# A two-layer hybrid transformer on one Trainium2 core: the delta rule's first doubling, the order of short TensorE products, and the convolution tiles

## The chip, the core and the metric

The kernel runs on one core of a Trainium2 chip. The metric is the device time of one execution in microseconds (us), as the median of several runs.

## The reference

Two layers, each made of a half-weighted SwiGLU, a mixer and a second half-weighted SwiGLU, with a layer norm after each. Layer 0 has the hybrid mixer (a gated delta rule beside a state-space scan), layer 1 the NSA mixer (compressed, selected and windowed attention). 256 tokens, width 1024, all in float32.

```python
def reference(...):
    h = x
    for layer in range(DEPTH):                       # DEPTH = 2
        h = layer_norm(ALPHA * h + 0.5 * swiglu(h, ffn_w_in[layer, 0], ffn_w_out[layer, 0]), ...)
        mix = hybrid_mixer(h, ...) if layer % 2 == 0 else nsa_mixer(h, positions, ...)
        h = layer_norm(ALPHA * h + mix, ...)
        h = layer_norm(ALPHA * h + 0.5 * swiglu(h, ffn_w_in[layer, 1], ffn_w_out[layer, 1]), ...)
    return h

def hybrid_mixer(x, w_in, ...):
    proj = x @ w_in                                  # split: gdn q,k,v | gdn z | b | a | ssd z | ssd x,B,C | dt
    o_a = gdn_branch(...)                            # silu(causal_conv(q,k,v)), then the gated delta rule
    o_b = ssd_branch(...)                            # silu(causal_conv(x,B,C)), then the scan
    return jnp.concatenate([o_a, o_b], axis=-1) @ w_out

# in gated_delta_rule, per head and chunk of tokens:
    a_low = where(strict lower triangle, (k * beta) @ k.T * decay, 0)
    sol = triangular_solve(a_low, rhs, lower=True, unit_diagonal=True)     # inverse of I + a_low
```

The causal convolution has four taps: each channel's output is a weighted sum of its projection at the token and the three before.

## The kernel before

Every weight is split into two fp32r parts, `whi` (rounded) and `wlo` (the rest), and so is the activation `x`. A float32 product is then three products on TensorE: high by high, high by low, low by high. The split is a ScalarE copy (or VectorE, as the planner decides) and a VectorE subtraction for each 128x1024 tile of weights.

**The planner.** No instruction is issued where it is written. A call like `nc.tensor.matmul` only records an operation (`Plan.add`). `Plan.order` then simulates all engines and picks, again and again, the operation that can start first, and among those of one engine that could start at once the one with the lowest priority number (its place in the recording). `price` is its cost table, `TURN` what it charges when TensorE goes from full to partial products (weights of 64 or fewer rows or columns). `Plan.emit` issues them in that order, which is why every row of the profile has one line, the line in `emit`. So a change of a price moves instructions and computes nothing else.

**The recording order** of a mixer comes from `weave`: it takes generators and always advances the one whose recorded TensorE cost divided by its weight is smallest. `W_HYB` are the weights for the hybrid's five: `delta` (delta rule), `space` (convolutions of v and of the state space), `gate` (the state space's z), `space2` (its scan), `out_a` (the first half of the output projection); `A_HYB` are head starts. `W_NSA` and `A_NSA` are those of the NSA mixer. `ORDER` adds random numbers to the priorities of a stage, here stage 4, the NSA mixer.

**Convolution tiles.** The hybrid has 28: 8 for q and k (`gdn_conv`, not woven with anything), 8 for v, 12 for the state space (both in `space`). A tile is 128 channels by 256 tokens, held in a PSUM bank, mostly `ps`, of which there are two. `proj_steps` computes it in 8 steps of three products of 256 columns. `conv_tile` then copies the bank to SBUF (`src`, part of a tile `cv`) on ScalarE, scales it by the last tap, adds the other three taps with three VectorE instructions, and applies SiLU on ScalarE.

**The inverse.** `delta` inverts 16 unit lower triangular 128x128 matrices (8 heads, two chunks) by doubling. Forward substitution on VectorE gives the inverses of all 16x16 diagonal blocks, `W`. From it two tiles are built: `Yd` (the inverse blocks) and `Xd` (their transposes), halves of one tile `XY` (`D2` in the code). The first doubling goes from 16x16 to 32x32 blocks with three sets of 64 products of 32x32 weights and 16 columns (four partition groups by 16 matrices): `pT` from the matrix and `Xd`, then `pY` and `pX` from `pT`, which correct `Yd` and `Xd`. In the profile they are `acc<-XY,AT`, `acc<-XY,TT` and `acc<-TT,XY` with 32x16. Each float32 product is two rows of the profile, each with a weight load. The next doublings (32x32 columns, then 64x64) follow in the same way.

**The start.** `spin(4, 4)` issues two products of 512 columns on ones, which nobody reads, while the first transfers are under way.

Of the kernel before, what the change touches and what calls it, by code (L numbers as in the profile page):

```python
# [45 lines left out]
    4: [(59170, 5.0, 1)],  # L46
}

ENDS = 3

# [8 lines left out]
A_HYB, A_NSA = (0.0, 10.0, 0.0, 0.0, 0.0), (0.0, -10.0, 0.0, -10.0)  # L59
W_HYB, W_NSA = (49.0, 114.0, 27.0, 19.0, 14.0), (122.0, 85.0, 81.0, 28.0)  # L60
# [127 lines left out]
class Op:  # L188
    __slots__ = ("eng", "fn", "args", "kw", "idx", "prio", "cost", "table", "deps", "succ", "ndep", "ready", "start",
                 "end", "alloc", "dense", "alts", "tiles", "nbytes", "quad", "port", "banks", "hot")  # L190


class Plan:
# [83 lines left out]
    def price(self, op, eng, fn, args, kw):  # L277
# [3 lines left out]
        if eng == "tensor":  # L281
            out, l, r = args[:3]
            if fn == "transpose":
                return max(l.ids.size * 2, r.ids.size) / 2.4 + 2
            N, M = r.ids.size, l.ids.size
            if l.dtype == F32R:
                return N / 2.4 + (13.5 if M > 32 else 7)
            if M <= 32:
                return N * 0.42 if l.p1 - l.p0 > 32 else max(20.0, N * 1.3)
            if M <= 64:  # L290
                return 58.0 if N <= 64 else max(109.0, N * 0.84)
            return 4 * max(N, M) / 2.4 + 9
# [63 lines left out]
    TURN = 150.0  # L356
# [3 lines left out]
    def order(self, caps):  # L360
        ops = self.ops
        for op in ops:
# [9 lines left out]
            op.banks = [] if op.eng == "tensor" else [t for t in op.tiles if t.space == "PSUM"]  # L372
            op.dense = op.eng == "tensor" and op.args[1].dtype == F32R and op.args[2].ids.size >= 256
# [17 lines left out]
        recent = []  # L391
        order = []
# [63 lines left out]
        while left:  # L456
            best = None
            for e in engs:
# [6 lines left out]
                for op in lst:  # L465
# [8 lines left out]
                    if e == "tensor":  # L474
                        if op.quad != partial:
# [24 lines left out]
            if eng == "tensor":  # L500
                partial = op.quad
                l, r = args[1:3]
# [95 lines left out]
class K:  # L598
# [307 lines left out]

    def proj_steps(self, x, w, ps):
# [328 lines left out]
    def conv_tile(self, ps, cw, off, n, c, bias, dst):  # L1236
# [5 lines left out]
        nc.scalar.activation(src, ps, AF.Copy)  # L1242
        self.plan.ops[-1].prio -= RANK
# [61 lines left out]
    def hybrid(self, x, then):  # L1305
# [75 lines left out]
        def gdn_conv(dests, banks=("ps", "ps")):  # L1381
            for n in range(0, len(dests), 2):
                w = self.col_tiles([w_col[c] for c, _ in dests[n:n + 2]])
                for e in range(2):
                    c, dst = dests[n + e]
                    ps = self.bank(banks[e])[:, :T]
                    yield from self.proj_steps(x, w[e], ps)
# [37 lines left out]
        def delta():  # L1425
# [56 lines left out]
            sw.append(self.m4(1024, "sw2"))  # L1482
            for w, dst, t in ((W, Yd, sw[0]), (W.rearrange("p r c -> p c r"), Xd, sw[2])):
                a, c = t[:, :512], t[:, 512:]
                for e in range(2):
                    V.tensor_scalar(a4(a)[:, :, e, :], w, hm[:, e:e + 1], None, OP.mult)
                V.transpose(c, a)
                self.copy(dst.rearrange("p k (a r) -> p k a r", a=2), c.rearrange("p (r a k) -> p k a r", r=16, a=2))
# [4 lines left out]
            yield  # L1493
            pT = self.bank("acc")
            for b, h, k in heads:
                for q in QS:
                    nc.tensor.matmul(pT[q, k * 16:k * 16 + 16], AT[b][q, h, q], Xd[q, k, :16], start=True, stop=True)
            V.tensor_scalar(Tt[:, :, :16], H3(pT[:, :256], 16), hm[:, 1:2], None, OP.mult)
            yield
            pX, pY = (t[:, :256] for t in (self.bank("acc"), self.bank("acc")))  # L1500
            for b, h, k in heads:
                for q in QS:
                    nc.tensor.matmul(pY[q, k * 16:k * 16 + 16], Tt[q, k, :], Yd[q, k, 16:], start=True, stop=True)
            for b, h, k in heads:
                for q in QS:
                    nc.tensor.matmul(pX[q, k * 16:k * 16 + 16], Yd[q, k, :], Tt[q, k, :16], start=True, stop=True)
            V.tensor_tensor(Yd[:, :, 16:], Yd[:, :, 16:], H3(pY, 16), OP.subtract)
            V.tensor_tensor(Xd[:, :, :16], Xd[:, :, :16], H3(pX, 16), OP.subtract)
# [3 lines left out]
            for b, h, k in heads:  # L1512
# [771 lines left out]
```

## Time and profile before

| what | value |
|---|---|
| median of 3 runs | 1071.63 us (1070.99 to 1073.05) |
| the profiled execution: its own time | 1072.49 us |
| the profiled execution: span in the profile | 1070.8 us |
| TensorE products (PE) busy | 1053.1 us, 98% |
| VectorE (DVE) busy | 1005.8 us, 94% |
| ScalarE (ACT) busy | 728.8 us, 68% |
| mean granted TensorE clock | 0.995 |

PE is TensorE's products, PEld its weight loads (they overlap), DVE is VectorE, ACT ScalarE, POOL GpSimd. Start times are in us from the start of the span. Products are pipelined, so the recorded length of one (283 ns for 256 columns) is longer than the distance to the next; costs below are taken from distances between starts. "<-issue" as the end of an idle time means that the profile shows nothing that was waited for.

### The profile page before, as it was taken

Reading aid. Unit: us, or ns where it says so; the run is one execution under the profiler, and the core shown is the slowest. Engines: PE = TensorE matmul, PEld = TensorE weight load, DVE = VectorE, ACT = ScalarE, POOL = GpSimd, SP = SyncE. Lnnn points to the kernel's source line nnn. Section 1 sums busy time; section 2 is a strip of 40 time slices with the busy share of each in tenths; the row PEclk is TensorE's granted clock in tenths of the full one; section 3 lists DMA queues with packets and bytes.
Section 4 is the critical chain, followed back from the end, with each engine's and each line's share of the span. In section 5 each row is a group of like instructions: output and inputs, shape, how many; then the busy total and the mean of one; then the engine's idle time right before and its main releaser. Section 6 shows DMA issues by size and latency. Waiting matters only on the chain.

```text
span 1070.8 us, 16409 instructions
## 1 busy us (share of the span) xinstructions
PE 1053.1 (98%) x6068; PEld 883.3 (82%) x6068; DVE 1005.8 (94%) x1433; ACT 728.8 (68%) x1162; POOL 70.6 (7%) x115
## 2 busy tenths in 40 slices
PE   9999999999989999999999999999999999999997
PEld 6888887898979888888887888888888778888885
DVE  6999999889979999999998999999988989999996
ACT  6678866389646765568875676678565887666770
POOL 0000000002001310000000000000101000000000
PEclk9999999999989999999999999999999999999999
DMA  9688867535522674378767647778662436477861
GB/s 369 225 274 237 254 220 278 176 115 206 161 99 91 217 254 176 135 252 257 233 221 254 212 142 237 230 240 266 207 222 69 151 112 222 148 228 233 258 194 40
DMA packets 64497, 217.30 MB, mean 203 GB/s; under 512 B 8560, under 2 KB 11296, under 8 KB 64416
## 3 DMA queue, kind: packets, MB, share of 16 engines
q1 hardware_dynamic: 59952, 200.25, 53.6%
q0 software_dynamic: 4320, 15.73, 8.2%
q8 instruction: 48, 0.79, 0.3%
q10 hardware_dynamic: 144, 0.26, 0.1%
q14 instruction: 33, 0.27, 0.1%
HBM read 213.96 MB, written 1.07 MB: 201 GB/s over the span
## 4 chain that ended last, share of the span: by engine, by line
PE 88%; DVE 6%; DMA 2%; ACT 1%; issue 1%; POOL 0%; SPq 0%; DVEq 0%; POOLq 0%; ACTq 0%
PE ps L574 42%; PE acc L574 32%; PE mp L574 14%; DVE wlo L574 1%; DMA raw<-in_hyb_w_tok_dram 1%; DVE arena L574 1%; DVE cv L574 1%; DMA DT<-rows 1%; DVE o L574 1%; DVE qs L574 0%; DMA X<-in_x_cols_dram 0%; ACT whi L574 0%; POOL arena L574 0%; ACT cv L574 0%; SPq L574 0%
## 5 line engine op out<-in xcount | busy, mean ns | idle before, releaser
L574 DVE TENSOR_TENSOR wlo<-raw,whi 128x1024 fp32r<-128x1024 f32 (+3 forms) x417 | 491.1, 1209 | 7.6 <-ACT whi L574 6.8
L574 ACT ACTIVATE whi<-raw 128x1024 fp32r<-128x1024 f32 (+2 forms) x430 | 429.5, 1047 | 89.0 <-DVE raw L574 73.2
L574 PE MATMUL ps<-whi,x 128*128 128x512 f32 (+1 forms) x864 | 233.5, 388 | 0.0
L574 PEld LDWEIGHTS ps<-whi,x 128*128 128x128 f32 x864 | 157.0, 188 | 29.1 <-issue 0.8
L574 DVE TENSOR_TENSOR raw<-raw,raw 128x1024 f32<-128x1024 f32 x128 | 152.6, 1218 | 0.0
L574 PE MATMUL ps<-wlo,x 128*128 128x512 f32 (+1 forms) x432 | 129.6, 387 | 0.0
L574 PE MATMUL ps<-x,whi 128*128 128x256 f32 (+2 forms) x560 | 115.8, 314 | 0.1
L574 PE MATMUL acc<-whi,gh 128*128 128x512 f32 x253 | 98.4, 392 | 0.6 <-ACT gh L574 0.6
L574 PE MATMUL acc<-whi,gl 128*128 128x512 f32 x253 | 98.4, 391 | 0.0
L574 PEld LDWEIGHTS ps<-x,whi 128*128 128x128 f32 (+1 forms) x560 | 91.6, 190 | 7.8 <-ACT cv L574 1.6
L574 PEld LDWEIGHTS ps<-wlo,x 128*128 128x128 f32 x432 | 79.3, 188 | 14.2 <-DVE wlo L574 0.2
L574 PE MATMUL acc<-wlo,gh 128*128 128x512 f32 x253 | 84.9, 391 | 0.0
L574 PE MATMUL ps<-x,wlo 128*128 128x256 f32 (+1 forms) x344 | 79.9, 285 | 0.0
L574 PE MATMUL acc<-whi,x 128*128 128x512 f32 x224 | 74.2, 408 | 1.0 <-ACT whi L574 1.0
L574 POOL DMA_DIRECT2D wlo<-in_ffn_w_out_dram x30 | 26.2, 873 | 555.8 <-ACT wlo L574 272.3
L574 PE MATMUL acc<-whi,g 128*128 128x512 f32 x192 | 61.0, 393 | 0.0
L574 PEld LDWEIGHTS ps<-x,wlo 128*128 128x128 f32 (+1 forms) x344 | 58.6, 191 | 1.2
L574 PEld LDWEIGHTS acc<-whi,gh 128*128 128x128 f32 x253 | 47.4, 188 | 10.3 <-ACT gh L574 0.8
L574 PEld LDWEIGHTS acc<-whi,gl 128*128 128x128 f32 x253 | 47.4, 188 | 10.1 <-DVE gl L574 0.4
L574 PEld LDWEIGHTS acc<-wlo,gh 128*128 128x128 f32 x253 | 47.4, 188 | 9.7
L574 PEld LDWEIGHTS acc<-whi,x 128*128 128x128 f32 x224 | 42.3, 193 | 11.1 <-ACT whi L574 2.6
L574 PE MATMUL ps<-whi,fhi 128*128 128x512 f32 x128 | 49.9, 390 | 0.0
(298 smaller groups left out, 1702.2 us busy)
## 6 DMA issues: line engine op xcount, KB each, us to landing
raw<-in_ffn_w_in_dram SPq DMA_DIRECT2D x175, 512.0 KB, 5.5
raw<-in_ffn_w_out_dram SPq DMA_DIRECT2D x88, 512.0 KB, 4.3
wlo<-in_ffn_w_out_dram POOLq DMA_DIRECT2D x30, 512.0 KB, 8.0
raw<-in_hyb_w_col_dram SPq DMA_DIRECT2D x28, 512.0 KB, 4.5
raw<-in_hyb_w_tok_dram SPq DMA_DIRECT2D x16, 512.0 KB, 8.4
raw<-in_hyb_w_out_dram SPq DMA_DIRECT2D x16, 512.0 KB, 3.8
raw<-in_nsa_w_tok_dram SPq DMA_DIRECT2D x8, 512.0 KB, 4.5
raw<-in_nsa_w_one_dram SPq DMA_DIRECT2D x8, 512.0 KB, 5.0
```

What stands on the lines that cost most here:

```text
L574: r = getattr(getattr(nc, eng), fn)(*[res(a) for a in args], **{k: res(a) for k, a in kw.items()})
```

## The change

1. **Convolution tiles.** `proj_two_steps` takes the place of `proj_steps`: for each of 8 steps the high part of the weights meets both parts of `x` in one product of 512 columns (two halves of the bank), then 8 products of 256 columns with the low part of the weights go to the first half. `conv_tile` copies the second half on ScalarE and adds the first on VectorE. 16 products a tile instead of 24, one VectorE add more.
2. **X by transposition.** `pX` and its subtraction go. `Xd` is made from `Yd` by a VectorE transposition of 32x32 blocks (`V.transpose` of one half of `D2` into the other), before the first doubling and again after `Yd` is corrected. `pT` and `pY` are recorded in two parts each, with a `yield` ahead, and two loops of the second doubling are written in one line.
3. **Spaced instructions.** The planner counts instruction words (4 for a float32 product, 2 for an fp32r one) and lets no 256 of them start within 3700 ns (`FETCH`).
4. **Prices.** Products with weights of 32 rows cost 17.5 ns up to 16 columns and 33 ns above; those with 33 to 64 columns of weights and up to 64 columns 117 instead of 58; `TURN` is 100 instead of 150.
5. **Numbers of the order.** `W_HYB`, `A_HYB`, `W_NSA`, `A_NSA` and the random numbers of stage 4 are new.
6. **One unread product more.** `spin(4, 4, 3)`: a third, of 384 columns.

```diff
 ORDER = {
-    4: [(59170, 5.0, 1)],
+    4: [(12984, 3.0, 8)],
 }
+FETCH = 256, 3700.0
-A_HYB, A_NSA = (0.0, 10.0, 0.0, 0.0, 0.0), (0.0, -10.0, 0.0, -10.0)
-W_HYB, W_NSA = (49.0, 114.0, 27.0, 19.0, 14.0), (122.0, 85.0, 81.0, 28.0)
+A_HYB, A_NSA = (0.0, 10.0, 0.0, 10.0, 20.0), (0.0, 0.0, 0.0, 0.0)
+W_HYB, W_NSA = (54.0, 86.0, 176.0, 65.0, 39.0), (62.0, 60.0, 198.0, 13.0)
...
+            if l.p1 - l.p0 <= 32:
+                return 17.5 if N <= 16 else 33.0
             if M <= 32:
-                return N * 0.42 if l.p1 - l.p0 > 32 else max(20.0, N * 1.3)
+                return N * 0.42
             if M <= 64:
-                return 58.0 if N <= 64 else max(109.0, N * 0.84)
+                return 117.0 if N <= 64 else max(109.0, N * 0.84)
-    TURN = 150.0
+    TURN = 100.0
...
+            op.words = 4 if op.eng == "tensor" and op.fn == "matmul" and op.args[1].dtype != F32R else 2
...
+        issued = [-1e9] * FETCH[0]
...
                     if e == "tensor":
+                        st = max(st, issued[op.words - 1 - FETCH[0]] + FETCH[1])
...
+                issued += [st] * op.words
+                del issued[:-FETCH[0]]
...
+    def proj_two_steps(self, x, w, ps):
+        mm = self.nc.tensor.matmul
+        for k in range(KD):
+            mm(ps, w[0][:, k, :], x[0][k // 2][:, k % 2].rearrange("p h b t -> p (h b t)"), start=k == 0, stop=False)
+            yield
+        for k in range(KD):
+            mm(ps[:, :T], w[1][:, k, :], self.xk(x, k)[0], start=False, stop=k == KD - 1)
+            if k % 2:
+                yield
...
         cv, src = self.pair("cv")
-        nc.scalar.activation(src, ps, AF.Copy)
-        self.plan.ops[-1].prio -= RANK
+        nc.scalar.activation(src, ps[:, T:], AF.Copy)
+        nc.vector.tensor_tensor(src, ps[:, :T], src, OP.add)
...
-                    ps = self.bank(banks[e])[:, :T]
-                    yield from self.proj_steps(x, w[e], ps)
+                    ps = self.bank(banks[e])
+                    yield from self.proj_two_steps(x, w[e], ps)
...
-            sw.append(self.m4(1024, "sw2"))
-            for w, dst, t in ((W, Yd, sw[0]), (W.rearrange("p r c -> p c r"), Xd, sw[2])):
-                a, c = t[:, :512], t[:, 512:]
-                for e in range(2):
-                    V.tensor_scalar(a4(a)[:, :, e, :], w, hm[:, e:e + 1], None, OP.mult)
-                V.transpose(c, a)
-                self.copy(dst.rearrange("p k (a r) -> p k a r", a=2), c.rearrange("p (r a k) -> p k a r", r=16, a=2))
+            for e in range(2):
+                V.tensor_scalar(a4(Z)[:, :, e, :], W, hm[:, e:e + 1], None, OP.mult)
+            V.transpose(Zt, Z)
+            self.copy(Yd.rearrange("p k (a r) -> p k a r", a=2), Zt.rearrange("p (r a k) -> p k a r", r=16, a=2))
+            V.transpose(D2[:, 512:], D2[:, :512])
...
+            pT, pY = self.bank("acc")[:, :256], self.bank("acc")[:, :256]
+            for part in (heads[:8], heads[8:]):
+                yield
+                for b, h, k in part:
+                    for q in QS:
+                        nc.tensor.matmul(pT[q, k * 16:k * 16 + 16], AT[b][q, h, q], Xd[q, k, :16], start=True, stop=True)
...
-            for b, h, k in heads:
-                for q in QS:
-                    nc.tensor.matmul(pX[q, k * 16:k * 16 + 16], Yd[q, k, :], Tt[q, k, :16], start=True, stop=True)
             V.tensor_tensor(Yd[:, :, 16:], Yd[:, :, 16:], H3(pY, 16), OP.subtract)
-            V.tensor_tensor(Xd[:, :, :16], Xd[:, :, :16], H3(pX, 16), OP.subtract)
+            V.transpose(D2[:, 512:], D2[:, :512])
...
-        spin(4, 4)
+        spin(4, 4, 3)
```

How the order moves, at two places. `acc` is the bank of the short products, `AT` the matrices, `TT` the corrected `pT`, `ps` a convolution tile's bank, `x` the activation, `whi` and `wlo` the weights; a number after a name tells tiles apart, the sizes are partitions by columns, and x32 at a row's end is a count of products. TensorE at the first doubling, before:

```order
L574 MATMUL acc_3107<-XY_3077,AT_484_2547 32x16 x32
L574 MATMUL acc_3107<-XY_3077,AT_503_2679 32x16 x32
L574 MATMUL ps_3176<-x_1747,whi_2942 128x256 x2
L574 MATMUL ps_3176<-x_1747,wlo_2989 128x256
L574 MATMUL ps_3176<-x_1747,whi_2942 128x256 x2
L574 MATMUL ps_3176<-x_1747,wlo_2989 128x256
L574 MATMUL acc_3185<-XY_3077,TT_2960 32x16 x64
L574 MATMUL acc_3259<-TT_2960,XY_3077 32x16 x64
```

and now, from the same product on:

```order
L583 MATMUL acc_2982<-XY_2957,AT_486_2480 32x16 x32
L583 MATMUL acc_2982<-XY_2957,AT_511_2621 32x16 x24
L583 MATMUL ps_2977<-x_1748,whi_2768 128x512
L583 MATMUL acc_2982<-XY_2957,AT_511_2621 32x16
L583 MATMUL ps_2977<-x_1754,whi_2768 128x512 x2
L583 MATMUL ps_2977<-x_1761,whi_2768 128x512 x2
L583 MATMUL ps_2977<-x_1764,whi_2768 128x512 x2
L583 MATMUL ps_2977<-x_1748,wlo_2794 128x256 x2
L583 MATMUL ps_2977<-x_1754,wlo_2794 128x256 x2
L583 MATMUL ps_2977<-x_1761,wlo_2794 128x256
L583 MATMUL acc_2982<-XY_2957,AT_511_2621 32x16 x7
```

The 64 products that stood together are now in runs of 56, 1 and 7 with a convolution tile between; those of `acc<-XY,TT` follow ten rows later in runs of 50, 1 and 13, and `acc<-TT,XY` 32x16 is gone.

VectorE at the same place (`cv` is a convolution tile in SBUF, three SCALAR_TENSOR_TENSOR its taps, `wlo` the subtraction of a split), before:

```order
L574 TENSOR_SCALAR TT_2960<-acc_3107,arena_144 128x16x16
L574 SCALAR_TENSOR_TENSOR cv_3038<-cv_3038,arena_144 128x254
L574 SCALAR_TENSOR_TENSOR cv_3100<-cv_3100,arena_144 128x254
L574 SCALAR_TENSOR_TENSOR cv_3038<-cv_3038,arena_144 128x253
L574 SCALAR_TENSOR_TENSOR cv_3100<-cv_3100,arena_144 128x253
L574 TENSOR_TENSOR wlo_3248<-raw_2985,whi_3051 128x1024
L574 TENSOR_TENSOR wlo_3308<-raw_3053,whi_3068 128x1024
L574 TENSOR_TENSOR XY_3077<-XY_3077,acc_3185 128x16x16
L574 TENSOR_TENSOR XY_3077<-XY_3077,acc_3259 128x16x16
```

and now:

```order
L583 TENSOR_SCALAR TT_2832<-acc_2982,arena_144 128x16x16
L583 SCALAR_TENSOR_TENSOR cv_3025<-cv_3025,arena_144 128x254
L583 TENSOR_TENSOR cv_3083<-ps_2977,cv_3083 128x256
L583 SCALAR_TENSOR_TENSOR cv_3025<-cv_3025,arena_144 128x253
L583 TENSOR_TENSOR wlo_3133<-raw_2962,whi_2980 128x1024
L583 SCALAR_TENSOR_TENSOR cv_3083<-cv_3083,arena_144 128x255
L583 TENSOR_TENSOR wlo_3160<-raw_3059,whi_3069 128x1024
L583 SCALAR_TENSOR_TENSOR cv_3083<-cv_3083,arena_144 128x254
L583 TENSOR_TENSOR cv_3171<-ps_3081,cv_3171 128x256
L583 SCALAR_TENSOR_TENSOR cv_3083<-cv_3083,arena_144 128x253
L583 TENSOR_TENSOR XY_2957<-XY_2957,acc_3091 128x16x16
L583 TENSOR_TENSOR wlo_3199<-raw_3135,whi_3153 128x1024
```

The adds that read a `ps` bank now stand in VectorE's queue between taps and splits, one of the two corrections of `XY` is gone, and a STREAM_TRANSPOSE of `XY` follows the last row here.

More of the change, by code (lines that the diff above doesn't have):

```diff
@@ L189 @@
     __slots__ = ("eng", "fn", "args", "kw", "idx", "prio", "cost", "table", "deps", "succ", "ndep", "ready", "start",
-                 "end", "alloc", "dense", "alts", "tiles", "nbytes", "quad", "port", "banks", "hot")
+                 "end", "alloc", "dense", "alts", "tiles", "nbytes", "quad", "port", "banks", "hot", "words")
 class Plan:
@@ L1492, in delta @@
             heads = [(b, h, b * 8 + h) for b in range(2) for h in range(8)]
-            yield
-            pT = self.bank("acc")
-            for b, h, k in heads:
-                for q in QS:
[L1497 to L1505, printed above, removed]
-                    nc.tensor.matmul(pX[q, k * 16:k * 16 + 16], Yd[q, k, :], Tt[q, k, :16], start=True, stop=True)
+            pT, pY = self.bank("acc")[:, :256], self.bank("acc")[:, :256]
[4 more added lines that the diff above has]
+                        nc.tensor.matmul(pT[q, k * 16:k * 16 + 16], AT[b][q, h, q], Xd[q, k, :16], start=True, stop=True)
+            V.tensor_scalar(Tt[:, :, :16], H3(pT, 16), hm[:, 1:2], None, OP.mult)
+            for part in (heads[:8], heads[8:]):
+                yield
+                for b, h, k in part:
+                    for q in QS:
+                        nc.tensor.matmul(pY[q, k * 16:k * 16 + 16], Tt[q, k, :], Yd[q, k, 16:], start=True, stop=True)
             V.tensor_tensor(Yd[:, :, 16:], Yd[:, :, 16:], H3(pY, 16), OP.subtract)
-            V.tensor_tensor(Xd[:, :, :16], Xd[:, :, :16], H3(pX, 16), OP.subtract)
+            V.transpose(D2[:, 512:], D2[:, :512])
             yield
@@ L1511, in delta @@
             pT = self.bank("acc")
-            for b, h, k in heads:
-                for u, v in pairs:
-                    nc.tensor.matmul(pT[v, k * 32:k * 32 + 32], AT[b][u, h, v], Xd[u, k, :], start=True, stop=True)
+            for (b, h, k), (u, v) in [(n, e) for n in heads for e in pairs]:
+                nc.tensor.matmul(pT[v, k * 32:k * 32 + 32], AT[b][u, h, v], Xd[u, k, :], start=True, stop=True)
             for u, v in pairs:
@@ L1520, in delta @@
             pX, pY = self.bank("acc"), self.bank("acc")
-            for b, h, k in heads:
-                for u, v in pairs:
-                    nc.tensor.matmul(pY[u, k * 32:k * 32 + 32], T5[v, k, :], Yd[v, k, :], start=True, stop=True)
+            for (b, h, k), (u, v) in [(n, e) for n in heads for e in pairs]:
+                nc.tensor.matmul(pY[u, k * 32:k * 32 + 32], T5[v, k, :], Yd[v, k, :], start=True, stop=True)
             for b, h, k in heads:
@@ L1661, in space @@
                     (w,) = self.col_tiles([w_col[16 + c]])
-                    ps = self.bank("ps")[:, :T]
-                    yield from self.proj_steps(x, w, ps)
+                    ps = self.bank("ps")
+                    yield from self.proj_two_steps(x, w, ps)
                     self.conv_tile(ps, cw, 64, 12, c, cw[:, 112 + c:113 + c], dst)
```

## The prediction

> **What bounds the kernel now.** I read the page first, for the share of each engine and the chain of waits, then short stretches of time over the whole span, then the stretch that stands out instruction by instruction. The page's head, its row of busy times and the chain that ended last:
>
> ```profile
> span 1070.8 us, 16409 instructions
> PE 1053.1 (98%) x6068; PEld 883.3 (82%) x6068; DVE 1005.8 (94%) x1433; ACT 728.8 (68%) x1162; POOL 70.6 (7%) x115
> PE 88%; DVE 6%; DMA 2%; ACT 1%; issue 1%; POOL 0%; SPq 0%; DVEq 0%; POOLq 0%; ACTq 0%
> ```
>
> TensorE is the chain: 88% of it, and idle for only 17.7 us of 1070.8. VectorE is close behind with 65 us idle. So what a TensorE edit saves is worth its full time only where VectorE can follow. Three long stretches (busy us of PE, PEld, DVE, ACT, POOL, then granted clock): the hybrid mixer with its edges, the feed-forward stage after it, the NSA mixer:
>
> ```profile
> 180.00:400.00 220.00, 214.13 (x1956) 192.95 (x1955) 201.94 (x404) 145.80 (x274) 24.00 (x34) 0.98 0.50 165
> 400.00:580.00 180.00, 179.64 (x835) 148.93 (x834) 176.32 (x202) 125.99 (x160) 8.08 (x9) 1.00 0.68 225
> 760.00:895.00 135.00, 134.29 (x875) 108.50 (x874) 119.75 (x239) 95.22 (x264) 12.25 (x30) 1.00 0.47 160
> ```
>
> Only the hybrid has TensorE idle in any amount (5.87 us) and a clock under 1.00. Four pieces of 4 us, same columns, place it:
>
> ```profile
> 292.00:296.00 4.00, 3.58 (x172) 2.97 (x170) 4.00 (x10) 1.00 (x3) 0.00 (x0) 1.00 0.79 292
> 296.00:300.00 4.00, 1.26 (x128) 1.16 (x128) 2.86 (x4) 1.67 (x3) 0.00 (x0) 0.94 0.26 98
> 300.00:304.00 4.00, 2.49 (x102) 2.46 (x103) 0.86 (x3) 0.42 (x2) 0.00 (x0) 0.50 0.02 4
> 304.00:308.00 4.00, 4.00 (x77) 3.75 (x77) 3.90 (x8) 1.83 (x4) 0.00 (x0) 0.71 0.01 4
> ```
>
> TensorE's rows there (start, length, count; in brackets the idle time before):
>
> ```profile
> 292.98 1.26 PE L574 MATMUL acc<-XY,AT 32*32 32x16 f32 x128
> 295.16 0.43 PE L574 MATMUL acc<-XY,TT 32*32 32x16 f32 x30
> 298.05 0.98 PE L574 MATMUL acc<-XY,TT 32*32 32x16 f32 x96 [2.46 <-issue]
> 298.90 0.41 PE L574 MATMUL acc<-TT,XY 32*32 32x16 f32 x28
> 301.51 1.57 PE L574 MATMUL acc<-TT,XY 32*32 32x16 f32 x98 [2.19 <-issue]
> 303.60 0.41 PE L574 MATMUL ps<-x,wlo 128*128 128x256 f32 x1
> 303.81 0.63 PE L574 MATMUL ps<-x,whi 128*128 128x256 f32 x2
> 304.24 0.41 PE L574 MATMUL ps<-x,wlo 128*128 128x256 f32 x1
> ```
>
> The reader is to see two gaps whose releaser is "issue": nothing in the trace was waited for. Between the gaps run 128 product rows (96 + 28 and four single ones), each with a weight load: 256 instructions in 1.26 us, then 2.19 us of nothing. A restart comes 3.46 us after the one before. I read that as TensorE having run out of instructions, which reach it 256 at a time. With products this short the supply is the bound.
>
> The Trainium skill (Runtime: NRT & Kernel Launch, section "Instruction fetch mechanics") says the same block size, 16 KiB or 256 instructions, but also that fetching is hidden and that crossing a block is "one DMA tail-bump, mostly hidden". The trace agrees on the size and not on the cost, 2.46 and 2.19 us. By that sentence the spacing would bring nothing; that is the third rival below.
>
> After the gaps the clock is 0.50, and a convolution step of three products takes 0.64 us (303.60 to 304.24).
>
> **The convolution tiles.** The old form, one tile to the next (first rows of two tiles), and the new one, which the first feed-forward stage already runs:
>
> ```profile
> 212.93 0.40 PE L574 MATMUL acc<-x,whi 128*128 128x256 f32 x2
> 215.81 0.40 PE L574 MATMUL ps<-x,whi 128*128 128x256 f32 x2
> ...
> 33.06 2.00 PE L574 MATMUL ps<-x,whi 128*128 128x512 f32 x8
> 34.90 1.11 PE L574 MATMUL ps<-x,wlo 128*128 128x256 f32 x8
> 35.85 2.00 PE L574 MATMUL ps<-x,whi 128*128 128x512 f32 x8
> ```
>
> 24 products take 2.88 us, the 8 + 8 that stream the same columns 2.79. Times 28 tiles (8 for q and k, 8 for v, 12 for the state space): 28 x 0.09 = -2.4 us, all on TensorE.
>
> The price is on VectorE. ScalarE's copy out of the bank stays one 256-column instruction, but a VectorE add of 256 columns is new in each tile. The feed-forward form has the same add, by chance 28 of them; beside it the rows for the other VectorE work that this change moves:
>
> ```profile
> L574 DVE TENSOR_TENSOR sg<-ps,sg 128x256 f32<-128x256 f32 x28 | 11.7, 419 | 0.3 <-ACT sg L574 0.3
> L574 DVE COPY XY<-sw x2: 602/622/642, 290.3 to 292.0; 128x512 f32<-128x512 f32 x2
> L574 DVE TENSOR_SCALAR sw<-sw,arena x5: 344/348/440, 268.7 to 289.9; 128x256 f32<-128x256 f32 x5
> L574 DVE STREAM_TRANSPOSE sw<-sw x3: 695/704/712, 267.7 to 290.8; 128x512 f32<-128x512 f32 x3
> L574 DVE COPY XT<-XY x1: 414/414/414, 304.2 to 304.2; 32x512 f32<-32x512 f32 x1
> 303.11 0.75 DVE L574 TENSOR_TENSOR XY<-XY,acc 128x256 f32<-128x256 f32 x2 [4.25 <-PE acc L574]
> ```
>
> 28 x 0.419 = +11.7 us as recorded; the last row shows that two neighbours of 256 columns overlap and cost 0.335 each, so +9.4 at least. Who frees the bank changes too: of two banks, a tile's is free for the tile after next only when VectorE, not ScalarE, has read it. In the feed-forward rows above TensorE goes through the same dependence without a gap while VectorE is full (25.00 of 25):
>
> ```profile
> 32.00:57.00 25.00, 25.00 (x127) 21.28 (x126) 25.00 (x36) 16.52 (x27) 0.00 (x0) 1.00 0.65 228
> ```
>
> **X by transposition.** The second product of the first doubling goes: 64 products, 128 rows. At the full clock these cost as the 96 rows above, 0.98 / 96 = 10.2 ns: -1.3 us on TensorE. On VectorE one subtraction (0.42), two multiplications (2 x 0.35) and one copy (0.62) go and one transposition more comes (two of XY and two of sw instead of three: +0.70): -1.0 us. By the order, the remaining copy of Y, one of kq and one of o went from VectorE to ScalarE (3 x 0.62, the kq and o copies priced by the nearest row: -1.9), and two 32-row copies into TT came to it (2 x 0.41 = +0.8). VectorE in all: +9.4 to +11.7, -1.0, -1.9, +0.8 = +7.3 to +9.6 us. ScalarE has 74 us idle in the stretch and takes the three copies for nothing; that idle time is their cover, and with it gone they would cost 1.9 us. The path from Y to the second doubling gains a transposition of 0.70 us, hidden as long as convolution products stand beside it; by the order they do.
>
> **Spaced instructions.** By the order no run of these products is longer than 57 (228 instructions), and 1 to 3 us of convolution products (rows of 0.12 to 0.23 us each) follow each run. 256 instructions then take longer than 3.46 us. Both gaps go: -2.46 - 2.19 = -4.65 us. With them goes the slow clock. It cost: 98 rows in 1.49 us (301.51 to the next start at 303.00) instead of 98 x 10.2 ns = 1.0, and five steps at 0.64 instead of 2.88 / 8 = 0.36: 0.5 + 1.4 = 1.9; with the broken step after them I take -2.0.
>
> **One unread product more.** Four rows of the warming product fill TensorE until the first real one:
>
> ```profile
> 1.07 3.78 PE L574 MATMUL acc<-ones 128*128 128x512 f32 x4 [1.07 <-POOL ones L574]
> 3.79 1.06 PE L574 MATMUL acc<-ones 128*128 128x512 f32 x1
> 5.87 2.08 PE L574 MATMUL acc<-whi,x 128*128 128x512 f32 x4 [1.02 <-ACT whi L574]
> ```
>
> The starts are (3.79 - 1.07) / 3 = 0.91 apart, so 384 columns, two rows, add about 2 x 0.68 = 1.36 us after 4.70: it ends near 6.06, up to 0.2 late. Against that, the first products at 5.87 run slow (four in 2.08), and a busier start may speed them. Bounds +0.2 and -0.7 (three products of 0.23, as in the eight from 33.06 to 34.90); weights still arrive by DMA there. I take -0.3.
>
> **Stage order.** In NSA the counts on TensorE don't change; only places do. The idle time before was 0.71 us, so little is to be won from waits; a worse order could cost as much as the waits that the hybrid showed. I take 0, ends -1 and +3. The weights of the hybrid's weave put the gate's products earlier; I price that inside the next step.
>
> **The sum.** TensorE alone: -2.4 - 1.3 - 4.65 - 2.0 = -10.35 in the hybrid. Can VectorE follow? It idled 220 - 201.94 = 18.06 us there. Shortened by 10.35 it has 7.7 left and must take 7.3 to 9.6 more. The stage after has 3.7 us idle in 180. So it would have to be busy without a break, which it is not anywhere in the mixer, since it waits for products and transfers at the stage's edges. I take 3 us of idle time as unavoidable, so 3 of the 10.35 come back as TensorE waits: -7.35. With the start: -7.65. Against the profiled execution's 1072.49 us (span 1070.8 and 1.7 around it) that is 1064.84. The median of the runs is 0.86 under the profiled one: 1064.0 us.
>
> **Rivals.**
> 1. VectorE isn't felt: the convolution's adds fit into the time that the gaps left, ScalarE takes more. Then -10.35 - 0.3, 1061.0. For it: outside the gaps the order before left TensorE only 5.87 - 4.65 = 1.2 us of waiting in the stretch. Against: the 7.7 us above.
> 2. VectorE holds the stage: idle time of 6 us stays, so the stage shortens by 18.06 - 6 - 9.6 = 2.5 and the time is 1069.
> 3. The gaps stay, because they are something other than the supply of instructions. Then only -2.4 - 1.3 - 0.3, 1067.6; VectorE has room for its adds in the gaps.
> 4. Slower: the bank wait. If VectorE's add comes late in its queue behind 1.2 us splits of weights, TensorE waits in every tile. It decides at 10.65 / 28 = 0.38 us per tile; at 0.55 us the time is 1076. Against it stand the feed-forward tiles above, which wait 0.
> 5. NSA's new order is worse by 3 us: 1067.
>
> **How the numbers follow.** Forecast 0.48, rival 1 0.24, rival 2 0.09, rival 3 0.07, rival 4 0.06, rival 5 0.06. 0.2% is 2.1 us, about what a measurement of this kernel can tell from no change. Rivals 1, 3 and 5 are faster; of rival 2 about half is within 0.2%; of rival 4 most is slower. Faster 0.88, same 0.07, slower 0.05. The range reaches from rival 1 with a good start and NSA (1059.0) to rival 2 (1069.0).
>
> **What the next profile would show.** Right: no "issue" wait over 1 us on TensorE between the two mixer edges; granted clock 1.00 throughout the hybrid; a convolution tile of 2.8 us; VectorE in the hybrid stretch above 97%; small TensorE waits on cv, wlo or XY of 2 to 4 us together. Wrong: gaps of 2 us still before 32x16 products; or TensorE waits for cv in most tiles, or NSA's TensorE idle time above 2 us.

## The result and the profile after

The changed kernel takes 1061.79 us (median of 4 runs, 1060.32 to 1063.61), the kernel before on the same chip 1072.27 (4 runs): ratio 0.9901 [0.9884, 0.9918], or 10.5 us less. The forecast was 1064.0 with a range of 1059.0 to 1069.0. The profiled execution took 1060.32 us (span 1058.6, granted clock 0.997); it was the fastest of the four, 1.5 us under their median, so the two profiles lie 12.2 us apart and not 10.5.

The page's busy times, beside which those of before stand in the prediction:

```profile
PE 1048.5 (99%) x5718; PEld 867.4 (82%) x5718; DVE 1008.7 (95%) x1457; ACT 732.2 (69%) x1169; POOL 71.4 (7%) x109
```

TensorE is busy 4.6 us less, in 350 rows fewer, and its idle time fell from 17.7 to 10.1 us. VectorE's busy time rose by only 2.9 us.

Each layer ends in a normalization with two aggregations on VectorE, one for each batch row. The start of the second one gives stage limits that stand in both traces (a stage is the time from one to the next, in us):

| stage | before | after | difference |
|---|---|---|---|
| start and first feed-forward | 187.69 | 185.19 | -2.50 |
| hybrid mixer | 228.64 | 218.32 | -10.32 |
| feed-forward 2 | 176.54 | 175.61 | -0.93 |
| feed-forward 3 | 175.33 | 176.50 | +1.17 |
| NSA mixer | 122.07 | 122.65 | +0.58 |
| feed-forward 4 | 173.83 | 173.69 | -0.14 |

All of it is the hybrid and the start; the other stages together are 0.7 longer. The hybrid in windows (busy us of PE, PEld, DVE, ACT, POOL; clock), first before, then after:

```profile
187.69:416.33 228.64, 222.77 (x1995) 200.29 (x1994) 210.10 (x415) 151.10 (x279) 23.98 (x34) 0.99 0.49 164
```

```profile
185.19:403.51 218.32, 217.90 (x1643) 185.25 (x1642) 210.56 (x433) 152.57 (x283) 27.91 (x34) 1.00 0.50 171
```

The reader is to see three things. TensorE was idle 5.87 us and now is 0.42. The clock is 1.00. And VectorE is busy for as long as before, 210.1 and 210.6 us, in 10 us less: its idle time went from 18.5 to 7.8. TensorE's rows at the place of the two gaps, in the trace after:

```profile
290.85 2.00 PE L583 MATMUL ps<-x,whi 128*128 128x512 f32 x8
292.69 1.11 PE L583 MATMUL ps<-x,wlo 128*128 128x256 f32 x8
293.65 0.39 PE L583 MATMUL ps<-x,whi 128*128 128x512 f32 x1
293.97 1.13 PE L583 MATMUL acc<-XY,AT 32*32 32x16 f32 x112
295.02 0.50 PE L583 MATMUL ps<-x,whi 128*128 128x512 f32 x1
295.46 0.23 PE L583 MATMUL acc<-XY,AT 32*32 32x16 f32 x2
295.62 1.65 PE L583 MATMUL ps<-x,whi 128*128 128x512 f32 x6
...
299.72 1.03 PE L583 MATMUL acc<-XY,TT 32*32 32x16 f32 x100
```

No row is preceded by idle time. The short products stand in pieces with convolution products between them, and a convolution tile takes 2.80 us (290.85 to 293.65). The waits of TensorE in the whole program (us in total, times, longest) are now five and sum to 2.4 us; those on `ones` and `whi`, at the start, are the only ones that were there before:

```profile
PE acc L583 <- POOL ones L583: 1.1, 1, 1.1
PE mp L583 <- DVE G L583: 0.4, 1, 0.4
PE acc L583 <- ACT whi L583: 0.4, 1, 0.4
PE acc L583 <- DVE gl L583: 0.3, 1, 0.3
PE mp L583 <- DVE PT L583: 0.2, 1, 0.2
```

### The profile page after: what moved, and what is told of

The parts are those of the page before. It is cut to its first block, busy times and chain, and to the rows that moved or that the text cites. A ratio compares the mean times of both kernels' runs of the same rounds, so it can differ in the third digit from the quotient of the medians.

```text
span 1058.6 us, 15724 instructions
## 1 busy us (share of the span) xinstructions
PE 1048.5 (99%) x5718; PEld 867.4 (82%) x5718; DVE 1008.7 (95%) x1457; ACT 732.2 (69%) x1169; POOL 71.4 (7%) x109
## 5 line engine op out<-in xcount | busy, mean ns | idle before, releaser
L583 PE MATMUL ps<-x,whi 128*128 128x512 f32 (+2 forms) x368 | 94.1, 383 | 0.0
L583 PEld LDWEIGHTS ps<-x,whi 128*128 128x128 f32 (+1 forms) x368 | 63.9, 185 | 11.4 <-issue 0.8
L583 PEld LDWEIGHTS acc<-whi,gl 128*128 128x128 f32 x253 | 47.3, 188 | 10.2 <-DVE gl L583 0.7
L583 PE MATMUL ps<-x,wlo 128*128 128x256 f32 (+1 forms) x344 | 55.2, 286 | 0.0
L583 PEld LDWEIGHTS ps<-x,wlo 128*128 128x128 f32 (+1 forms) x344 | 49.0, 188 | 3.7
L583 PEld LDWEIGHTS acc<-whi,x 128*128 128x128 f32 x224 | 41.6, 188 | 10.1 <-ACT whi L583 1.3
```

The costliest lines, as they stand in the source:

```text
L583: r = getattr(getattr(nc, eng), fn)(*[res(a) for a in args], **{k: res(a) for k, a in kw.items()})
```

## Experiments

Each expectation names its own theories A, B and C. Behind them stand the prediction's mechanisms and sizes (instructions reach TensorE in blocks of 256; the gaps, the tiles and the product each bring what the sum says) and three rivals: the gaps are something else; or VectorE decides; or the new weave numbers do. In each batch the kernel before ran too, at 1072.3 to 1072.4 us.

**The spacing taken out of the changed kernel.**

```diff
-FETCH = 256, 3700.0
+FETCH = 256, 0.0
```

> The changed kernel with the planner's 3700 ns rule set to 0. TensorE now has 64 products of 32x16 (256 instructions with their weight loads), six convolution products of 512 columns (about 1.4 us), and 64 such products again. Theory A (TensorE gets its instructions 256 at a time, one block about 3.5 us after the one before): a gap without a releaser of 1.5 to 2.4 us within the second run, perhaps a smaller one at the 32x32 products, and a slower clock if the pause is long enough; 1.5 to 5 us over the changed kernel's 1061.8. Theory B (the gaps of before came from something else than the rate of instructions, such as the product of X that is gone): no gap, within 1 us of 1061.8.

Measured 1066.93 us, ratio 0.996 [0.9947, 0.9973]: 5.1 us over the changed kernel. TensorE's short products there:

```profile
294.23 1.26 PE L583 MATMUL acc<-XY,AT 32*32 32x16 f32 x128
296.77 0.66 PE L583 MATMUL acc<-XY,TT 32*32 32x16 f32 x57
299.59 1.15 PE L583 MATMUL acc<-XY,TT 32*32 32x16 f32 x71 [2.16 <-issue]
```

and the window behind them:

```profile
300.00:310.00 10.00, 10.00 (x235) 8.45 (x228) 6.32 (x13) 4.92 (x10) 0.00 (x0) 0.69 0.10 25
```

One gap is back, 2.16 us, and the clock is 0.69 over the ten microseconds after it. The hybrid takes 225.41 us instead of 218.32, so gap, slow clock and what comes late behind them cost more than the gap alone. Theory A is confirmed at the upper end of its price.

The traces also hold the supply itself. DMA queue 8 carries only instructions, 16384 bytes a transfer. Its rows (transfers, MB, share of the 16 engines' span) in the page before, in the page after, and in the window of 295 to 302 us before, which holds the two gaps:

```profile
q8 instruction: 48, 0.79, 0.3%
```

```profile
q8 instruction: 45, 0.74, 0.3%
```

```profile
q8 instruction: 2, 0.03, 1.7%
```

TensorE ran 12237 products and weight loads before and 11532 after, which is 47.8 and 45.05 blocks of 256; in all fourteen kernels the count of transfers is that quotient to the nearest whole. And in each of the twelve gaps over 0.4 us with "issue" as their releaser, in seven kernels, TensorE went on 1.28 to 1.59 us after such a transfer had landed. Before, these transfers started at 295.74 and 299.17 and took 0.92 and 0.97 us; TensorE went on at 298.05 and 301.51. That is direct evidence for the supply of instructions.

**A long run of short products, to measure the supply by itself.** Without the spacing, and with 256 products more into a bank that nothing reads:

```diff
-FETCH = 256, 3700.0
+FETCH = 256, 0.0
...
+            more = self.bank("acc")[:, :256]
+            for _ in range(4):
+                for b, h, k in heads:
+                    for q in QS:
+                        nc.tensor.matmul(more[q, k * 16:k * 16 + 16], Tt[q, k, :], Yd[q, k, 16:], start=True, stop=True)
```

> The changed kernel without the spacing, and with 256 more 32x16 products in one piece behind pY's second half, into a bank that nothing reads. 64 products are 128 rows and 256 instructions and take 1.26 us when nothing holds them. Theory A (instructions reach TensorE in blocks of 256, each about 3.46 us after the one before): a gap of 2.1 to 2.3 us after every 128 rows, four of them, restarts 3.4 to 3.5 us apart, the piece takes 13 to 14.5 us and the kernel 1076 to 1082. Rival (a gap is a single event at this place of the program): one gap, the piece takes 7 to 8 us, the kernel 1070 to 1074.

Measured 1087.28 us in one run. The rows:

```profile
297.37 0.66 PE L583 MATMUL acc<-XY,TT 32*32 32x16 f32 x57
298.59 1.25 PE L583 MATMUL acc<-XY,TT 32*32 32x16 f32 x128 [0.55 <-issue]
303.41 1.90 PE L583 MATMUL acc<-XY,TT 32*32 32x16 f32 x128 [3.58 <-issue]
307.14 1.90 PE L583 MATMUL acc<-XY,TT 32*32 32x16 f32 x128 [1.83 <-issue]
311.14 1.90 PE L583 MATMUL acc<-XY,TT 32*32 32x16 f32 x128 [2.10 <-issue]
315.14 1.15 PE L583 MATMUL acc<-XY,TT 32*32 32x16 f32 x71 [2.10 <-issue]
```

and the window over them:

```profile
298.00:318.00 20.00, 9.84 (x593) 9.16 (x590) 5.37 (x9) 2.18 (x5) 0.00 (x0) 0.62 0.11 30
```

The gaps come after every 128 rows exactly (256 instructions with the weight loads), which settles the block; a single event at that place of the program is out. The cost was 20.4 us over the kernel without spacing (1066.93), of which the added products are some 5.2 (512 rows of 10.2 ns). It is above what I expected, for two reasons in the rows: the restarts lie 3.73 to 4.82 us apart instead of 3.46, and at a clock of 0.62 a block's rows take 1.90 instead of 1.26 us. So the spacing between restarts isn't fixed. The instruction transfers show what it is made of: in the three later rounds the next transfer starts 1.09 to 1.14 us after a restart, takes 1.18 to 1.41 us, and the restart follows 1.45 to 1.52 us after it has landed. The gap of 3.58 us had its transfer 2.59 us after the restart; why is open.

**The spacing alone, in the kernel before.**

```diff
+FETCH = 256, 3700.0
...
+                        st = max(st, issued[op.words - 1 - FETCH[0]] + FETCH[1])
```

> The kernel before with the 3700 ns rule alone; the product of X stays. Theory A (supply of instructions): both gaps (2.46 and 2.19 us) and the slow clock after them (about 2.0 us) go, TensorE's work stays: 6.0 to 6.7 us faster than before, near 1066. Theory B (the gaps are something else): they stay, within 1.5 us of before.

Measured 1074.63 us, 1.0022 [1.0013, 1.003]: slower, where theory A expected a gain of 6. The gaps did go, but for one of 0.7 us, and the clock stayed at 1.00 there. The windows, then the longest waits of the whole program:

```profile
290.00:320.00 30.00, 28.32 (x723) 25.32 (x722) 27.75 (x46) 17.18 (x33) 2.18 (x2) 1.00 0.42 138
360.00:370.00 10.00, 7.78 (x37) 5.96 (x35) 9.14 (x19) 4.21 (x9) 6.67 (x20) 0.83 0.54 179
```

```profile
PE mp L581 <- DVE o L581: 2.2, 1, 2.2
PE mp L581 <- DVE vg L581: 2.1, 1, 2.1
```

The time came back later, as waits for VectorE: 2.2 us for `o` near 362 with a slow clock behind it (0.83 in the second window), 2.1 for `vg` in the next stage. I read that as VectorE having caught up in TensorE's gaps, and being late without them. The trace doesn't bear this out: ahead of both waits VectorE itself stood idle, for a GpSimd result (`arena`) and for a ScalarE copy whose weights had come late by DMA:

```profile
360.21 0.17 DVE L581 TENSOR_TENSOR arena<-arena 128x8 f32<-128x8 f32 x1 [1.54 <-POOL arena L581]
569.45 1.06 ACT L581 ACTIVATE whi<-raw 128x1024 fp32r<-128x1024 f32 x1 [5.86 <-DMA raw<-in_ffn_w_in_dram]
570.54 2.58 DVE L581 TENSOR_TENSOR wlo<-raw,whi 128x1024 fp32r<-128x1024 f32 x2 [2.16 <-ACT whi L581]
```

So it is the place of a few steps in the order that came to hurt, and not that VectorE had too much to do; why they came late with the spacing isn't shown. The next experiments change the order's numbers.

**The hybrid's old weave numbers in the changed kernel.**

```diff
-A_HYB = (0.0, 10.0, 0.0, 10.0, 20.0)
+A_HYB = (0.0, 10.0, 0.0, 0.0, 0.0)
-W_HYB = (54.0, 86.0, 176.0, 65.0, 39.0)
+W_HYB = (49.0, 114.0, 27.0, 19.0, 14.0)
```

> The changed kernel with the hybrid's weave weights and head starts of before. Theory A (VectorE has no idle time left, and only the new weights, which put the gate's products early beside VectorE's densest work, let it follow): TensorE waits for wlo or cv, 2 to 5 us slower than 1061.8. Theory B (the weights hardly matter): within 1 us.

Measured 1071.37 us, 0.9993 [0.9984, 1.0002]: seven numbers that differ take 9.6 of the 10.5 us away, about twice what theory A expected. TensorE's largest wait, and its, VectorE's and ScalarE's rows at the longest:

```profile
PE ps L583 <- DVE cv L583: 3.5, 4, 2.2
```

```profile
265.38 3.65 PE L583 MATMUL ps<-x,whi 128*128 128x512 f32 x8 [2.22 <-DVE cv L583]
...
263.34 1.65 DVE L583 SCALAR_TENSOR_TENSOR AT<-DT,arena,kq 128x128 f32<-128x128 f32 x6
264.91 0.41 DVE L583 TENSOR_TENSOR cv<-ps,cv 128x256 f32<-128x256 f32 x1
...
264.17 0.38 ACT L583 ACTIVATE cv<-ps 128x256 f32<-128x256 f32 x1
```

This is a bank wait, as in the fourth rival: the tile's add (264.91) stood behind six multiplications of the delta rule in VectorE's queue, and the bank wasn't free. But ScalarE's copy of the bank's other half, which the add needs, came only at 264.17, a microsecond after TensorE had stopped (263.16). An add right behind it would have freed the bank only some 0.4 us sooner; the larger part of this wait is ScalarE's. (The change also took away the raised priority that this copy had; no run tried that alone.) The wait of 2.22 us then slowed the eight products after it from 2.00 to 3.65 us.

**The new weave numbers alone, in the kernel before** (the two lines above, the other way round).

> The kernel before with one edit: the hybrid's new weave numbers (A_HYB, W_HYB), nothing else. Theory A (the numbers are found for one set of products, spacings and VectorE work, and are worth nothing elsewhere): no gain, 1072 to 1076 us, the two gaps with issue as their releaser stay. Theory B (the new numbers are simply better, the change's gain is mostly theirs): 1064 to 1067 us, with less TensorE waiting than the 17.7 us of before.

Measured 1077.28 us, 1.0047 [1.0034, 1.006]: 5 us slower than with the old ones, a little over theory A's range, and with one gap of 3.6 us "issue" instead of the two. The numbers are not better as such.

**Spacing and new weave numbers in the kernel before.**

> The kernel before with the spacing rule and the hybrid's new weave numbers; the products, the block transposition and VectorE's work stay those of before. Spacing alone measured 1074.6. Theory A (the numbers fit only the change's own set of work): 1070 to 1075 us, the time of the gaps back as TensorE waits for VectorE. Theory B (spacing plus weights that let VectorE follow is what brings the gain): 1066 us or less, about the 6.6 us of the two gaps and the slow clock behind them, no wait over 1 us in the hybrid.

Measured 1070.30 us, 0.9984 [0.9975, 0.9993]. That is 4.3 less than spacing alone, and 2 less than before; seen from before, most of the roughly 6.6 us of the gaps and the slow clock still doesn't arrive. But against the same numbers without spacing (1077.28) the rule is worth 7.0 us here, and with the old numbers it cost 2.4: what the spacing brings hangs on the order around it. No wait is over 1.2 us, the hybrid's clock is 1.00, and TensorE's small waits and its 24-product tiles remain. A's range holds the time, but the long waits for VectorE that A named aren't there.

**The old convolution tiles in the changed kernel, with the new and with the old weave numbers.** The raised priority of ScalarE's copy stays out in both.

```diff
-        nc.scalar.activation(src, ps[:, T:], AF.Copy)
-        nc.vector.tensor_tensor(src, ps[:, :T], src, OP.add)
+        nc.scalar.activation(src, ps, AF.Copy)
...
-                    yield from self.proj_two_steps(x, w, ps)
+                    yield from self.proj_steps(x, w, ps)
```

> The changed kernel with the convolution tiles of before: 24 products of 256 columns a tile, no add on VectorE. Theory A (TensorE bounds the hybrid): 28 x 0.09 = 2.4 us slower, 1064.2. Theory B (VectorE bounds it, 28 adds of 0.34 to 0.42 us = 9.4 to 11.7 us of its work go): no slower, or faster by up to 3 us. As the planner lays the order anew, 1 us either way tells nothing.

> The changed kernel with the convolution tiles of before (three products a step, no VectorE add) and the hybrid's weave numbers of before; X by block transposition, one product less and the spacing stay. With the new tiles the old numbers measured 1071.4, with the new numbers the old tiles 1065.7. Theory A (the old numbers are bad because TensorE waits for the new VectorE add in the convolution tiles): without the add they are as good as the new ones, 1064 to 1067 us, no wait of TensorE on cv. Theory B (they are bad for the rest, the spaced doubling, too): 1069 to 1073 us, waits on other VectorE results of 2 us or more.

With the new numbers 1065.65 us (0.9944 [0.9931, 0.9956]), 3.9 more than the changed kernel, so theory B of the first is out; with the old ones 1067.09 (0.995 [0.9938, 0.9963]), at the edge of theory A's range of the second. Together with the two above:

| spaced, X transposed | old weave numbers | new weave numbers |
|---|---|---|
| old tiles | 1067.09 | 1065.65 |
| new tiles | 1071.37 | 1061.79 |

With the old tiles the numbers matter 1.4 us, with the new ones 9.6. The new tiles cost 4.3 with the old numbers and bring 3.9 with the new. (The 1.4 isn't clear of the intervals.) So it is the new tile, with its add and a bank that two engines must read, that the numbers make room for in this kernel. They do more than that elsewhere: in the kernel before with spacing, which has the old tiles, they were worth 4.3. With the old numbers and tiles TensorE has no wait on VectorE's `cv`; its largest is this:

```profile
PE mp L583 <- DVE y L583: 1.6, 3, 1.0
```

**A second VectorE add in every convolution tile** (it writes a place that is written again):

```diff
+        nc.vector.tensor_tensor(cv, ps[:, :T], src, OP.add)
```

> The changed kernel with VectorE's add of each convolution tile made twice (the second result is overwritten): 28 more VectorE instructions of 0.34 to 0.42 us, 9.4 to 11.7 us, and each bank read later. VectorE has 7.7 us idle in the hybrid stretch of the changed kernel. Theory A (VectorE is close behind TensorE): the stage grows by 2 to 6 us, with TensorE waits for wlo or cv. Theory B (VectorE's idle time and ScalarE take it up): within 1 us.

Measured 1072.02 us, 1.0001 [0.9991, 1.0012]: +10.2 us; the hybrid grew by 9.0, more than theory A's 2 to 6. VectorE's busy time rose by 11.0, and TensorE waits for it in the tiles (the page's busy times, then the largest wait):

```profile
PE 1053.1 (98%) x5718; PEld 867.8 (81%) x5718; DVE 1019.7 (95%) x1489; ACT 729.3 (68%) x1163; POOL 72.0 (7%) x109
```

```profile
PE ps L583 <- DVE cv L583: 3.3, 2, 2.3
```

So the added work was felt almost one to one, and VectorE's idle time in the hybrid stayed where it was (7.35 us, 7.76 in the changed kernel), as if there were no room left. It isn't a price per microsecond, though. The old tiles, which take the 28 adds away, brought nothing back. And each of these kernels has an order laid anew, with numbers found for another set of work, and here the bank is also read twice; no run separates these from the work itself.

**The second product of the first doubling put back.**

```diff
+            sw.append(self.m4(1024, "sw2"))
+            for w, dst, t in ((W, Yd, sw[0]), (W.rearrange("p r c -> p c r"), Xd, sw[2])):
...
+                        nc.tensor.matmul(pX[q, k * 16:k * 16 + 16], Yd[q, k, :], Tt[q, k, :16], start=True, stop=True)
...
-            V.transpose(D2[:, 512:], D2[:, :512])
+            V.tensor_tensor(Xd[:, :, :16], Xd[:, :, :16], H3(pX, 16), OP.subtract)
```

> The changed kernel with the 64 products that correct X put back, spaced like the others, and X built as before; the transpositions of XY go. Theory A (TensorE bounds the hybrid and the products cost 10.2 ns a row): 128 rows, 1.3 us slower than 1061.8. Theory B (only the gaps counted; products that stand between others cost nothing, or VectorE's transpositions cost as much): within 0.5 us. Theory C (each switch between short and full products costs extra): 2 us or more slower.

Measured 1063.85 us, 0.9918 [0.9905, 0.9932]: +2.1, with intervals that overlap those of the changed kernel, so neither A's 1.3 nor C's 2 or more is excluded.

**NSA's old numbers** (`ORDER`, `A_NSA`, `W_NSA` of before).

> The changed kernel with the weave weights, head starts and random numbers of before for the NSA mixer; prices and spacing stay. Theory A (NSA's new numbers are worth nothing, its stage moved by +0.6 us between the two profiles): within 1.5 us of 1061.8, NSA's stage within 1.5 us. Theory B (the numbers matter because they were found for the new prices): 2 to 5 us slower.

Measured 1066.36 us, 0.994 [0.9926, 0.9953]: +4.6. The NSA stage takes 129.39 us instead of 122.65, and 122.07 before; its largest waits:

```profile
PE mp L583 <- DVE PT L583: 1.9, 2, 1.1
PE mp L583 <- ACT PT L583: 1.2, 1, 1.2
```

Under the changed prices and spacing rule the old numbers give a worse order of this stage, and the new ones only repair that: theory B. With the spacing alone, old prices and old numbers the stage took 122.04 us, and 123.37 in the run with new hybrid numbers, so the spacing by itself isn't what makes it worse; that leaves the prices, alone or with it.

**Two unread products instead of three.**

> The changed kernel with two unread products at the start instead of three. Theory A (the third keeps TensorE busy until the first real product, so that the clock is up earlier): the low products of the first stage start 1.0 to 1.3 us later again and the time is 0.7 to 1.3 us over 1061.8. Theory B (the start is bound by the transfers of the weights, so the stage only waits elsewhere): less than 0.4 us.

Measured 1062.99 us, 0.9919 [0.9905, 0.9932], +1.2, which the intervals don't separate from nothing. The traces say more. The first four real products, in this kernel and in the kernel before with spacing, which also has two unread products:

```profile
5.89 2.08 PE L583 MATMUL acc<-whi,x 128*128 128x512 f32 x4 [1.04 <-ACT whi L583]
```

```profile
5.79 1.25 PE L581 MATMUL acc<-whi,x 128*128 128x512 f32 x4 [1.12 <-ACT whi L581]
```

With two unread products they took 2.08 us in three profiles and 1.25 in two. With three it was 1.24 to 1.65 in all nine. The trace's clock record begins, with 1.00, at 4.3 to 6.8 us in the eleven profiles with 1.24 to 1.65 and at 9.4 to 10.7 in the three with 2.08. So the third product makes sure of a start that came about by chance before. The next bank begins at 17.0 to 17.4 us in those eleven and at 18.5, 19.1 and 19.1 in the three. Over many executions that is some 1 us (1.7 x 3/5), estimated from few profiles.

## Why the prediction was right, and where not

- **The supply of instructions** is shown: in blocks of 256, gaps of about 2.1 us after 128 rows, a gap back without the spacing, and an instruction transfer that lands ahead of every restart. The Trainium skill (Runtime: NRT & Kernel Launch, section "Instruction fetch mechanics") has the block size, which the runs confirm, and "mostly hidden", which they contradict for products this short. The third rival is out. With its slow clock the rule is worth 5.1 us in the changed kernel, where one gap would be left, against 6.65 in the sum for two; in the kernel before it cost 2.4 us with the old numbers and brought 7.0 with the new.
- **The tiles** are 2.80 us as forecast. 28 x 0.09 is 2.5 and not the 2.4 of the sum. Undone they cost 3.9 us; the product 2.1 instead of 1.3. Both are over the forecast, neither outside what the intervals allow.
- **The hybrid's TensorE sum** was -10.35, the stage shortened by 10.32. That the two agree so closely is in part luck: TensorE's idle time fell by 5.45 us where the gaps were put at 4.65, and its busy time by 4.87 where tiles, product and slow clock were put at 5.7. The prediction then gave 3 us back, and that step failed: TensorE waits 0.42 us in the stage. What was wrong is VectorE's term. I had +7.3 to +9.6 us of work; the stage shows +0.5 (210.10 to 210.56). The adds came as priced, but three weight splits moved out of the stage, and convolution taps, copies and block building fell. After, in the stage:

```profile
L583 DVE TENSOR_TENSOR wlo<-raw,whi 128x1024 fp32r<-128x1024 f32 x60 | 73.2, 1233 | 0.3
L583 DVE SCALAR_TENSOR_TENSOR cv<-cv,arena 128x255 f32<-128x255 f32 x28 | 13.3, 476 | 0.1
L583 DVE SCALAR_TENSOR_TENSOR cv<-cv,arena 128x253 f32<-128x253 f32 x28 | 13.1, 472 | 0.0
L583 DVE TENSOR_TENSOR cv<-ps,cv 128x256 f32<-128x256 f32 x24 | 9.9, 413 | 0.5 <-ACT cv L583 0.4
L583 DVE TENSOR_TENSOR cv<-acc,cv 128x256 f32<-128x256 f32 x4 | 1.7, 419 | 0.1
```

  and before, the splits and the same taps:

```profile
L574 DVE TENSOR_TENSOR wlo<-raw,whi 128x1024 fp32r<-128x1024 f32 x63 | 76.2, 1225 | 0.2
L574 DVE SCALAR_TENSOR_TENSOR cv<-cv,arena 128x253 f32<-128x253 f32 x28 | 14.1, 507 | 0.1
L574 DVE SCALAR_TENSOR_TENSOR cv<-cv,arena 128x255 f32<-128x255 f32 x28 | 13.9, 501 | 2.9 <-ACT cv L574 2.6
```

  So the adds' +11.6 us met -3.0 from the splits and -1.6 from these taps. The delta rule's `o` fell by 1.0, copies of XY, `kq` and `o` by 2.6 and the building of the blocks in `sw` by 1.5, while transpositions of XY and copies into TT came to 2.8. That leaves +4.7. The lengths of all VectorE instructions of the stage, added up, rise by 3.2 us; the rest down to +0.5 is overlap of neighbouring instructions. I don't divide it further. The 3 us of idle time that I took as unavoidable were no row but a guess, and VectorE at 96.4% of the stage stays below the 97% that I named as the sign, as do TensorE's waits below the 2 to 4 us.
- **Rival 1** (1061.0) comes nearest to the time, and in the changed kernel its mechanism holds: VectorE isn't felt (0.42 us of TensorE waits), its added work fits into the time that the gaps left, and ScalarE has taken over copies. The prediction gave it 0.24, half of what it gave the forecast. What the rival doesn't say is how narrowly this holds: other order numbers or a second add bring 9.6 and 10.2 us back.
- **The weave numbers** were the larger error of reasoning. The prediction gave them half a sentence, "price that inside the next step". They cost 5 us alone in the kernel before and bring 4.3 there with spacing, 1.4 with the old tiles, and 9.6 here, and they decide between the forecast and a kernel no faster than before. The fourth rival's mechanism, the bank wait, is real (3.5 us of waits on `cv`, the longest 2.2, of which ScalarE's late copy is the larger part), and a chance of 0.06 was right only because the numbers came with the change. The feed-forward tiles that I held against it said nothing about the hybrid's queue.
- **NSA** at 0 came true (+0.58), but as the balance of a loss (4.6 us) and its repair, neither of which the prediction saw.
- **The start** was put at -0.3, with bounds +0.2 and -0.7. In the two profiles the second bank comes 1.26 earlier, which is outside. The step that failed is the clock: I let three products run 0.23 us faster each, where the first eleven took 4.40 us before (from 5.87 on) and 2.97 after (from 6.02 on). Of the other 1.2 us of the first stage's -2.50, 1.0 was waits at its end (0.6 on ScalarE's `gh`, 0.4 on `vg`), which some profiles of both kinds show; I put them down to the execution, not to the edit.

What stays open: the transposition was never undone alone. From the kernel before with spacing (1074.63) to the one with old tiles and numbers (1067.09) lie 7.5 us, of the transposition, the product, the third unread product, the new prices and NSA's numbers together. The product's 2.1 and the start's 1 leave some 4.4 that the runs don't divide; the stages place them in the hybrid (230.17 to 224.23) and in the one after (179.88 to 176.32). These hold the waits for `o` and `vg` of the kernel with spacing, each with a slow clock behind it, so the order may be most of it. Nor was it tried how long the instructions must be spaced at least.

## What to carry to other kernels

Where two engines are both over 90% busy, what a removed gap is worth hangs on the order around it: removing the two gaps alone made this kernel slower, with other order numbers the same rule was worth 7 us, and in the changed kernel 5. Price a change of order numbers as a term of its own, by what stands in the other engines' queues at the moment when a bank must come free, and expect to find such numbers again after every change of prices. Short TensorE products belong in pieces of fewer than 256 instructions (here at most 112 rows, 224 instructions), with longer products between them. Before you call an engine too busy, look at whether it was itself idle just ahead of the wait, and for what.

## What the runs showed of the hardware

**Instructions.** They reached TensorE by transfers of 16384 bytes, 256 at a time. When short products had used up a block, TensorE stood still until 1.28 to 1.59 us after the next transfer had landed (twelve gaps). A fixed time between blocks isn't the rule: at the lower clock of the long run the gap stays near 2 us while the block takes longer.

**The clock.** The cost of a TensorE wait can be larger than the wait. Eight products took 3.65 us instead of 2.00 after the bank wait of 2.22, so it cost 3.9 there, and the ten-microsecond windows behind such waits show 0.83 and 0.69. But a wait of 2.35 us in the kernel with the second add (297.05 to 299.40) cost no clock:

```profile
295.06:298.47 3.41, 1.99 (x13) 1.63 (x11) 3.41 (x11) 2.33 (x4) 0.00 (x0) 1.00 0.40 142
298.47:301.88 3.41, 2.48 (x13) 2.19 (x14) 3.18 (x10) 2.41 (x4) 0.00 (x0) 1.00 0.29 100
```

The difference is where the wait lies. Within a trace the granted clock changes only a whole number of 3.41 us apart (before: at 9.35, 299.48 and 306.31, which is 85 and 2 times 3.413). Dividing each span into such stretches gives one rule for all fourteen traces: from the full clock it fell to 0.50 after a stretch in which TensorE was idle for 1.60 to 2.98 us (nine falls within the program, in seven kernels), and never after one with 1.42 or less. The wait of 2.35 us lay across two stretches, with 1.42 and 0.93 idle; that of 2.22 lay almost whole in one. So a wait of 2 us costs nearly twice its length if it falls into one stretch, and only itself if it is cut in two. The Trainium skill (TensorE: Matmul & The Clock Gate, section "What's actually happening") puts the idle, half-rate clock after an idle window of about 3.4 us; the stretches here have that length, but 1.60 us of idle time in one was enough.
